# A transformer layer's feed-forward in seven products for each 2x2 grid of blocks, with activations spilled to DRAM

## The chip, the core and the metric

The kernel runs on one core of one Trainium2 chip. TensorE (PE) multiplies and writes PSUM, VectorE (DVE) and ScalarE (ACT) work elementwise, GpSimd (POOL) and SyncE (SP) mainly issue DMAs. The metric is device time in microseconds (us) of one execution. Lower is better.

## The reference

One layer of a diffusion backbone over 512 latent tokens and 256 context tokens of width 2048, all in float32. Cut to what matters:

```python
x = x + gt_m * (concatenate([hg_lat, at_lat], -1) @ w_out)       # mixers, output projection
h = modulate(rms_norm(x, norm_ffn_g), sh_f, sc_f)                # (512, 2048)
gate, up = split(h @ w_gate_up, 2, axis=-1)                      # w_gate_up (2048, 2 * 5632)
x = x + gt_f * ((silu(gate) * up) @ w_down)                      # w_down (5632, 2048)
```

Ahead of these lines stand the modulation (six rows of 2048 from silu(c) @ w_mod), a first norm, one input projection, a gated recurrence over eight heads and a windowed attention over eight heads. The change touches little of that.

## The kernel before

Every large product is made of three passes over fp32r operands. An operand a is split into a high part (rounded by ScalarE, function `split`) and a low part (a minus the high part, VectorE), and `mm3` adds high x high, high x low and low x high in one PSUM bank. PSUM has eight banks of 512 columns, four under the name mm and four under aux.

`Weights` loads weights in tiles of 512 KB on SP's DMA queue (tile wr), splits them in parts of 512 columns (wh, wl) and keeps a few parts ahead. `proj_a` multiplies activations (stationary) with weights (moving), a bank for each tile of 128 tokens; `proj_b` multiplies weights (stationary) with activations (moving, 512 tokens), a bank for each block of 128 columns. All products of the large projections are 512 columns wide, but for those of the context (256 tokens) and of the first gate of the feed-forward, which is made in two halves of 256 tokens.

Order of the stages: modulation and norm; context states of the recurrence; attention; recurrence of four pairs of heads; output projection in two halves of eight K chunks each, `add_gated` multiplying each bank by the gate (tile tm) and adding it to x1, which stays in SBUF (512 x 2048); the second norm `h2_half` for two tiles of tokens at a time (squares on ScalarE, a reciprocal root `rsqrt` of fourteen small VectorE steps, transposes on TensorE, modulation on ScalarE, split on VectorE); the feed-forward.

The feed-forward runs over blocks of two groups of 512 columns: gate (silu on ScalarE into sg), up (times sg, split into sa2), then down for all 2048 output columns in four parts of 512, each added to x1 with its gate. In the last block each finished tile of x1 is sent to the output. The four gate rows for it (tile gt_row) are made by `mod_row` in `mod_lane` during the first block: each is 16 VectorE operations on tiles m_w that SP loads, summed over partitions by one product.

Small work is woven into the products by `Lane`, which asks an estimate of the engines' clocks whether a next step may be issued. The framework that places instructions on the engines' queues may move an instruction ahead of others that it doesn't depend on; the trace shows the order that came out.

Of the kernel before, what the change touches and what calls it, by code (L numbers as in the profile page):

```python
# [9 lines left out]
F32 = mybir.dt.float32  # L10
# [8 lines left out]
P = 128  # L19
D = 2048  # L20
# [90 lines left out]
class Timed:  # L111
    """An engine whose calls are estimated."""
# [50 lines left out]
def tile_block(ctx: ExitStack, tc: tile.TileContext, x, c, ctx_in, c_ctx, w_mod, b_mod, norm_mix_g,  # L163
# [28 lines left out]
    gtm_d = dram.tile([1, D], F32, name="gtm_d")  # L192

    # ---------------------------------------------------------------- constants
# [12 lines left out]
    def rsqrt(tmp, v, shape, tag, eng=None, bufs=2):  # L207
        """1 / sqrt(v) by Newton's iteration from the usual bit-level seed."""
# [12 lines left out]
    # columns of small vectors: cols[d, j] = v[j * 128 + d]  # L221
# [40 lines left out]
    def lower_bounds(lt):  # L262
        """first row of a softmax over the layers; lbc[:, dir * 8 + head]"""
# [16 lines left out]
    # ---------------------------------------------------------------- products in three single passes  # L280
# [10 lines left out]
    class Weights:  # L291
        """Weight tiles [128, G, N] in the order of their use: loads and splits run ahead of the products."""
# [7 lines left out]
        def add(self, w, rows, c0, N, G):  # L300
            """G chunks of rows in a load, 512 columns in all in a split"""
# [14 lines left out]
        def ahead(self, upto):  # L316
            """splits issued for parts below upto, loads for as many more as there are buffers"""
# [54 lines left out]
    def proj_a(ws, rows, hT, toks, N, evac, before=None):  # L372
        """[tok, cols]: one bank for each tile of 128 tokens; rows: K chunks in order"""
# [15 lines left out]
    def proj_b(ws, hT, n_tok, N, evac, t0=0):  # L389
        """[cols, tok]: blocks of 128 columns, 512 / n_tok of them in a bank"""  # L390
# [22 lines left out]
    # ---------------------------------------------------------------- first part: modulation, h, keys and values  # L413
# [51 lines left out]
        # silu(c), silu(c_ctx)  # L465
# [144 lines left out]
    for grp in ff_blocks:  # L610
        for fg in grp:
            for c0 in (0, 0, D_FF) if fg == 0 else (0, D_FF):
                ws.add(w_gate_up, all_k, c0 + 512 * fg, 512, 2)
# [893 lines left out]
```

## Time and profile before

| | |
|---|---|
| time, median of 3 runs | 2664.23 us (2660.33 to 2671.72) |
| span of the profiled execution | 2664.4 us |
| TensorE busy | 2610.7 us, 98% |
| VectorE busy | 1494.4 us, 56% |
| ScalarE busy | 912.5 us, 34% |
| GpSimd busy | 89.1 us, 3% |
| read from and written to HBM | 368.5 MB and 14.7 MB |

The page gives the span alone for the profiled execution; it lies within 0.2 us of the median. A busy TensorE means that some product was in flight, not that products followed each other as fast as they can, so it is read together with the number of products in a stretch. Records of one product overlap with those of the next, so the price of a product is the distance between starts, not the mean length of a record.

### The profile page before, as it was taken

What the parts mean: (1) busy time and instruction counts of PE and PEld (TensorE: products, weight loads), DVE (VectorE), ACT (ScalarE), POOL (GpSimd) and SP (SyncE); (2) the same over time, 40 slices, a digit from 0 to 9 for tenths busy, and PEclk for the clock granted to TensorE, in tenths of its full rate; (3) what the DMA queues carried; (4) which work ended last, traced back from release to release, by engine and by line L of the source; (5) the groups of instructions that cost most, each with busy time, mean ns of one, the idle gap of its engine ahead of it and who ended that gap; (6) DMA issues with size and microseconds to landing.
All of it is one profiled execution on the core that took longest, in us unless ns stands there. A gap on an engine that the chain in (4) does not pass through costs nothing.

```text
span 2664.4 us, 33786 instructions
## 1 busy us (share of the span) xinstructions
PE 2610.7 (98%) x12495; PEld 2137.4 (80%) x12495; DVE 1494.4 (56%) x3085; ACT 912.5 (34%) x1781; POOL 89.1 (3%) x245
## 2 busy tenths in 40 slices
PE   7999999999999999999999999999999999999999
PEld 4579887878888878788788888888888888888887
DVE  4468967787888886567744333433353334233425
ACT  4245444447433343335222222222322222222222
POOL 0000010000011021000000000000000000000000
PEclk9999999999999999999999999999999999999999
DMA  9978677761323335546742332333223322332233
GB/s 345 319 258 268 217 234 223 231 193 59 113 81 102 98 119 190 165 139 202 243 139 96 95 95 95 99 99 95 95 95 96 97 98 97 95 95 95 96 103 111
DMA packets 230199, 385.36 MB, mean 145 GB/s; under 512 B 13201, under 2 KB 78898, under 8 KB 229266
## 3 DMA queue, kind: packets, MB, share of 16 engines
q1 hardware_dynamic: 210336, 354.48, 41.2%
q10 hardware_dynamic: 15682, 16.85, 1.9%
q0 software_dynamic: 4016, 11.88, 1.5%
q8 instruction: 98, 1.61, 0.2%
q14 instruction: 67, 0.55, 0.1%
HBM read 368.46 MB, written 14.69 MB: 144 GB/s over the span
## 4 chain that ended last, share of the span: by engine, by line
PE 84%; DVE 6%; DMA 4%; issue 3%; ACT 2%; POOL 1%; SPq 0%; ACTq 0%; DVEq 0%; POOLq 0%
PE mm L127 77%; PE aux L127 7%; DMA m_w<-in_w_mod_dram 2%; DVE wl L127 1%; DVE m_acc L127 1%; ACT hT L127 1%; DVE h L127 1%; DMA wr<-in_w_in_dram 0%; DMA mraw<-mix_d 0%; ACT wh L127 0%; DVE ce L127 0%; DMA ring<-in_ctx_dram 0%; POOL rs_t L127 0%; DVE tm L127 0%; DVE x L127 0%
## 5 line engine op out<-in xcount | busy, mean ns | idle before, releaser
L127 DVE TENSOR_TENSOR wl<-wr,wh 128x512 fp32r<-128x512 f32 x920 | 623.2, 688 | 904.7 <-PE mm L127 469.6
L127 ACT ACTIVATE wh<-wr 128x512 fp32r<-128x512 f32 x920 | 569.7, 630 | 1289.2 <-PE mm L127 1155.0
L127 PE MATMUL mm<-h,wh 128*128 128x512 f32 (+1 forms) x2944 | 880.6, 382 | 0.7 <-ACT wh L127 0.6
L127 PEld LDWEIGHTS mm<-h,wh 128*128 128x128 f32 x2944 | 544.0, 188 | 110.1 <-issue 1.7
L127 PE MATMUL mm<-h,wl 128*128 128x512 f32 (+1 forms) x1472 | 563.2, 383 | 1.8 <-DVE wl L127 1.8
L127 PE MATMUL mm<-wh,sa 128*128 128x512 f32 x1408 | 434.4, 389 | 0.0
L127 PEld LDWEIGHTS mm<-h,wl 128*128 128x128 f32 x1472 | 276.1, 188 | 61.0 <-DVE wl L127 2.5
L127 PEld LDWEIGHTS mm<-wh,sa 128*128 128x128 f32 x1408 | 264.3, 188 | 55.0
L127 PE MATMUL mm<-wh,hT 128*128 128x512 f32 x896 | 297.0, 402 | 3.0 <-ACT hT L127 3.0
L127 PE MATMUL mm<-wl,sa 128*128 128x512 f32 x704 | 273.9, 389 | 0.0
L127 PE MATMUL mm<-hT,wh 128*128 128x512 f32 x768 | 246.6, 397 | 0.0
L127 DVE SCALAR_TENSOR_TENSOR m_acc<-m_w,c_col,m_acc 128x512 f32<-128x512 f32 x240 | 179.6, 748 | 60.8 <-DMA m_w<-in_w_mod_dram 58.6
L127 PEld LDWEIGHTS mm<-wh,hT 128*128 128x128 f32 x896 | 169.2, 189 | 54.7 <-issue 8.6
L127 PE MATMUL mm<-wl,hT 128*128 128x512 f32 x448 | 178.4, 398 | 0.0
L127 PE MATMUL mm<-wh,mT 128*128 128x512 f32 x512 | 165.4, 398 | 4.2 <-DVE gsig L127 2.3
L127 PEld LDWEIGHTS mm<-hT,wh 128*128 128x128 f32 x768 | 142.2, 188 | 28.3
L127 PEld LDWEIGHTS mm<-wl,sa 128*128 128x128 f32 x704 | 132.2, 188 | 27.5
L127 PE MATMUL mm<-hT,wl 128*128 128x512 f32 x384 | 151.9, 396 | 0.0
L127 PEld LDWEIGHTS mm<-wh,mT 128*128 128x128 f32 x512 | 96.9, 189 | 28.5 <-DVE tm L127 4.1
L127 PEld LDWEIGHTS mm<-wl,hT 128*128 128x128 f32 x448 | 84.7, 189 | 24.0 <-issue 6.1
L127 PE MATMUL mm<-wl,mT 128*128 128x512 f32 x256 | 101.0, 394 | 0.0
L127 PE MATMUL mm<-cT,wh 128*128 128x256 f32 x512 | 93.5, 284 | 0.5 <-ACT wh L127 0.5
(251 smaller groups left out, 2301.9 us busy)
## 6 DMA issues: line engine op xcount, KB each, us to landing
wr<-in_w_gate_up_dram SPq DMA_DIRECT2D x184, 512.0 KB, 3.5
wr<-in_w_in_dram SPq DMA_DIRECT2D x144, 512.0 KB, 4.4
m_w<-in_w_mod_dram SPq DMA_DIRECT2D x128, 512.0 KB, 4.6
wr<-in_w_down_dram SPq DMA_DIRECT2D x88, 512.0 KB, 3.6
ring<-in_w_mod_dram SPq DMA_DIRECT2D x64, 512.0 KB, 8.8
wr<-in_w_out_dram SPq DMA_DIRECT2D x36, 512.0 KB, 4.2
wr<-in_w_in_dram ACTq DMA_DIRECT2D x16, 256.0 KB, 6.0
ring<-in_x_dram SPq DMA_DIRECT2D x4, 1024.0 KB, 8.8
```

Of the source, the lines that this page charges most:

```text
L127: return f(*a, **k)
```

## The change

The feed-forward is written anew by the Winograd form of Strassen's scheme. The grid for gate and up: tokens in two halves of 256, K in two halves of 1024, columns in gate and up (the two halves of w_gate_up). A group is 256 columns of both, there are 22; it takes eight steps (K chunk s of the first half with chunk s + 8 of the second), and each step makes seven products of blocks, `PRODUCTS`, each as 2 x 3 passes of 256 columns, into seven PSUM banks. For that VectorE makes four sums of the four weight blocks in three operations (`st_sums`), ScalarE the high parts of seven blocks (`st_high`, 1792 elements a partition), VectorE the low parts (`st_low`). The raw weights have three buffers (tag fx, shared with the raw activations xa), high and low parts three each. The activations are turned by f32 products with a diagonal of the norm (`turn`), summed and split (`form`) beside the first group. `evac_up` combines the seven banks, takes the silu, multiplies, makes sums and parts of the result for down and writes them to DRAM (sf_d, on POOL's queue).

Down does the same over 22 K chunk pairs, in four spans of 6, 6, 5 and 5 steps, for four column parts each; the sets come back from sf_d into eight buffers as these become free. `evac_down` combines seven banks and writes the part into y_d in DRAM: the first span writes, the second and third add by DMA, the last one adds in SBUF what `prepare_down` made of y_d, x1 and the gate, and sends the result out.

Ahead of it: x1 is also written to DRAM (x1_d), the squares of the second norm are taken in `add_gated` on ScalarE, the norm waits for all four tiles of tokens, and the four gate rows of the feed-forward join the earlier `mod_tasks` (buffer m_r single, in its own pool) and are stored in gtf_d. `h2_half`, the feed-forward's `Weights` and its lane work are gone.

```diff
+SC = 256
+N_UP = D_FF // SC
+SPANS = (6, 6, 5, 5)
+    def mod_gate(j, c0, dst):
+        t = est.tile(mp, [P, 512], F32, "m_r", "m_r", 1)
+        yield from mod_row(mp, c0 + 512 * j, t)
+        pool.dma_start(dst[0:1, 512 * j:512 * j + 512], t[0:1, :])
+        yield
+    mod_tasks += [mod_gate(j, 5 * D, gtf_d) for j in range(4)]
...
             dve.tensor_tensor(tm, bank, gate, op=ALU.mult)
+            dve.tensor_tensor(x1[j][:, t, :], x1[j][:, t, :], tm, op=ALU.add)
+            if squares:
+                act.activation(tm, x1[j][:, t, :], AF.Square, accum_out=ssj[:, t, j:j + 1])
+                if t == NT - 1:
+                    pool.dma_start(x1_d[:, 512 * j:512 * j + 512].rearrange("(t p) d -> p t d", p=P), x1[j])
...
+    PRODUCTS = ((0, 0), (2, 2), (5, 5), (3, 4), (1, 6), (4, 3), (6, 1))
+    def st_load(i):
+            u.x = est.tile(fx, [P, 8, SC], F32, "fx", "fx", 3)
+            for h in range(2):
+                sp_q.dma_start(u.x[:, 2 * h:2 * h + 2, :], u.src[h])
+    def st_sums(i):
+            dve.tensor_tensor(xx[:, 4:6, :], xx[:, 0:1, :].to_broadcast([P, 2, SC]), xx[:, 1:3, :], op=ALU.add)
+            dve.tensor_tensor(xx[:, 6, :], xx[:, 4, :], xx[:, 2, :], op=ALU.add)
+            dve.tensor_tensor(xx[:, 7, :], xx[:, 6, :], xx[:, 3, :], op=ALU.add)
+    def st_high(i):
+            u.hi = est.tile(fx, [P, 7, SC], F32R, "fh", "fh", 3)
+            act.activation(u.hi, u.x[:, 1:8, :], AF.Copy)
+    def st_low(i):
+            u.lo = est.tile(fx, [P, 7, SC], F32R, "fl", "fl", 3)
+            dve.tensor_tensor(u.lo, u.x[:, 1:8, :], u.hi.bitcast(F32), op=ALU.subtract)
...
+    def turn(s, h):
+        if h == 0:
+            xa[s] = est.tile(fx, [P, 8, SC], F32, "fx", "fx", 3)
+        kc = s + 8 * h
+        pt = aux_bank()
+        for n, t in enumerate((2, 3, 0, 1)):
+            pe.matmul(pt[:, n * P:(n + 1) * P], x1[kc // 4][:, t, (kc % 4) * P:(kc % 4 + 1) * P], diag[:, t, :],
+                      start=True, stop=True, skip_group_check=True)
+        act.activation(xa[s][:, 2 * h:2 * h + 2, :], pt.rearrange("p (h t) -> p h t", h=2), AF.Identity,
+                       bias=ab2[:, 1, kc:kc + 1], scale=ab2[:, 0, kc:kc + 1])
+    def form(s):
+        new_set(s)
+        a_sums(xa[s])
+        act.activation(sets[s][0], xa[s][:, 1:8, :], AF.Copy)
+        dve.tensor_tensor(sets[s][1], xa[s][:, 1:8, :], sets[s][0].bitcast(F32), op=ALU.subtract)
+    def evac_up(g, banks):
+        p1, p2, p6, p7, q4, q5, p3 = banks
+        e = est.tile(xg, [P, 4, 512], F32, "big", "big", 4)
+        r, u0, t, u1 = (e[:, k, :] for k in range(4))
+        act.activation(r, p1, AF.Copy)
+        dve.tensor_tensor(u0, p2, r, op=ALU.add)
+        dve.tensor_tensor(r, p6, r, op=ALU.add)
+        dve.tensor_tensor(t, r, p7, op=ALU.subtract)
+        dve.tensor_tensor(u1, t, q4, op=ALU.add)
+        dve.tensor_tensor(r, q5, r, op=ALU.subtract)
+        dve.tensor_tensor(t, q5, t, op=ALU.subtract)
+        dve.tensor_tensor(r, p3, r, op=ALU.add)
+        act.activation(t, t, AF.Silu)
+        act.activation(r, r, AF.Silu)
+        yield
+        dve.tensor_tensor(xx[:, 0:4:2, :], hf(t), hf(u1), op=ALU.mult)
+        dve.tensor_tensor(xx[:, 1:4:2, :], hf(r), hf(u0), op=ALU.mult)
+        yield
+        a_sums(xx)
+        act.activation(hl[0], xx[:, 1:8, :], AF.Copy)
+        yield
+        dve.tensor_tensor(hl[1], xx[:, 1:8, :], hl[0].bitcast(F32), op=ALU.subtract)
+        for i in range(2):
+            pool.dma_start(sf_d[2 * g + i].bitcast(F32), hl[i].bitcast(F32).rearrange("p f n -> p (f n)"))
+        yield
...
+    def evac_down(j, b, banks):
+        def done(k):
+            if fin:
+                dve.tensor_tensor(ck, ck, gt[:, n:n + 1, :].to_broadcast([P, 2, SC]), op=ALU.mult)
+                dve.tensor_tensor(c[:, k, :], c[:, k, :], z[:, k, :], op=ALU.add)
+                sp_q.dma_start(rows_of(out, h, n, j), ck)
+            elif b == 0:
+                pool.dma_start(rows_of(y_d, h, n, j), ck)
+            else:
+                pool.dma_start(rows_of(y_d, h, n, j), ck, accum_op=ALU.add)
...
+    for i, u in enumerate(steps):
+        st_load(i + 3)
+        st_sums(i + 2)
+        st_high(i + 2)
+        if i < 8:
+            hooks = {0: lambda: turn(i + 1, 0), 3: lambda: turn(i + 1, 1)}
+        run_step(i, hooks)
+        form(i + 1)
+        st_low(i + 2)
+        if not u.up and u.b == len(SPANS) - 1 and u.first:
+            tail.append(prepare_down(u.g))
+        for g in list(tail):
+            if next(g, tail) is tail:
+                tail.remove(g)
+        if u.last:
+            g = evac_up(u.g, u.banks) if u.up else evac_down(u.g, u.b, u.banks)
+            next(g)
+            tail.append(g)
+        if last_use[u.a] == i and pending:
+            n = pending.pop(0)
+            new_set(n)
+            for k in range(2):
+                pool.dma_start(sets[n][k].bitcast(F32).rearrange("p f n -> p (f n)"), sf_d[2 * (n - 8) + k].bitcast(F32))
```

## Rows read from the trace of the kernel before

**Rows 1.** The page's first lines, with busy time, share and instructions.

```profile
span 2664.4 us, 33786 instructions
PE 2610.7 (98%) x12495; PEld 2137.4 (80%) x12495; DVE 1494.4 (56%) x3085; ACT 912.5 (34%) x1781; POOL 89.1 (3%) x245
```

**Rows 2.** Windows: us, busy (count) of each engine, PEclk, DMA share, GB/s.

```profile
0.00:100.00 100.00, 83.12 (x471) 48.99 (x471) 47.85 (x125) 38.64 (x61) 1.16 (x7) 0.97 1.03 345
700.00:800.00 100.00, 97.95 (x475) 82.69 (x474) 90.46 (x256) 36.18 (x77) 12.09 (x34) 0.98 0.29 90
900.00:1000.00 100.00, 96.08 (x468) 79.79 (x468) 85.66 (x217) 39.35 (x90) 14.92 (x42) 0.98 0.35 109
1600.00:2000.00 400.00, 400.00 (x1756) 329.45 (x1755) 153.50 (x229) 105.78 (x170) 0.00 (x0) 1.00 0.30 97
1194.00:2660.00 1466.00, 1460.07 (x6594) 1206.77 (x6592) 618.69 (x980) 407.61 (x667) 0.00 (x0) 1.00 0.34 111
```

**Rows 3.** Timeline of TensorE between output projection and feed-forward.

```profile
1190.82 0.39 PE L127 MATMUL mm<-wh,mT 128*128 128x512 f32 x1
1192.95 2.23 PE L127 MATMUL aux<-ident,xn 128*128 128x128 f32 x16 [1.74 <-issue]
1194.98 1.01 PE L127 MATMUL mm<-h,wh 128*128 128x256 f32 x3
```

**Rows 4.** Timeline of TensorE, the context's projections: start, us, work merged.

```profile
224.74 0.40 PE L127 MATMUL mm<-cT,wh 128*128 128x256 f32 x2
228.63 0.40 PE L127 MATMUL mm<-cT,wh 128*128 128x256 f32 x2
235.13 1.02 PE L127 MATMUL aux<-m_acc,ones 128*128 128x512 f32 x2
236.22 0.28 PE L127 MATMUL mm<-cT,wl 128*128 128x256 f32 x1
```

**Rows 5.** Groups with shapes apart: busy us, mean ns, idle before, releaser.

```profile
L127 DVE TENSOR_TENSOR wl<-wr,wh 128x512 fp32r<-128x512 f32 x920 | 623.2, 688 | 904.7 <-PE mm L127 469.6 <-ACT wh L127 434.1
L127 DVE TENSOR_TENSOR h<-h,h 128x256 fp32r<-128x256 f32 x32 | 12.4, 416 | 0.1
L127 ACT ACTIVATE wh<-wr 128x512 fp32r<-128x512 f32 x920 | 569.7, 630 | 1289.2 <-PE mm L127 1155.0 <-DMA wr<-in_w_in_dram 37.8 <-PE aux L127 35.9
L127 ACT ACTIVATE xn<-x 128x2048 f32<-128x2048 f32 x4 | 7.6, 1911 | 0.0
L127 DVE SCALAR_TENSOR_TENSOR m_acc<-m_w,c_col,m_acc 128x512 f32<-128x512 f32 x240 | 179.6, 748 | 60.8 <-DMA m_w<-in_w_mod_dram 58.6
```

**Rows 6.** Timeline of VectorE: independent and dependent operations in sequence.

```profile
774.98 0.41 DVE L127 TENSOR_TENSOR ky<-hf,ky 128x256 f32<-128x256 f32 x1
775.32 0.41 DVE L127 TENSOR_TENSOR ky<-kx,hP 128x256 f32<-128x256 f32 x1
...
1179.00 0.69 DVE L127 TENSOR_TENSOR tm<-mm,gt_c 128x512 f32<-128x512 f32 x1
1179.73 0.69 DVE L127 TENSOR_TENSOR x<-x,tm 128x512 f32<-128x512 f32 x1
1180.35 0.69 DVE L127 TENSOR_TENSOR wl<-wr,wh 128x512 fp32r<-128x512 f32 x1
```

**Rows 7.** Timeline of VectorE inside the reciprocal root of the second norm.

```profile
1186.03 0.16 DVE L127 TENSOR_TENSOR rs_t<-rs_y 128x2 f32<-128x2 f32 x1
1186.11 0.68 DVE L127 TENSOR_TENSOR wl<-wr,wh 128x512 fp32r<-128x512 f32 x1
1186.71 0.15 DVE L127 TENSOR_TENSOR rs_t<-rs_t,ss 128x2 f32<-128x2 f32 x1
```

**Rows 8.** Window of TensorE: us, busy (count), PEclk, DMA share, GB/s.

```profile
420.00:440.00 20.00, 16.58 (x71) 0.88 0.68 216
```

**Rows 9.** DMA issues: out, in, engine, count, KB each, median us to landing.

```profile
wr<-in_w_gate_up_dram SPq DMA_DIRECT2D x184, 512.0 KB, 3.5
```

**Rows 10.** Timeline of VectorE, the last operation.

```profile
2660.53 0.69 DVE L127 TENSOR_TENSOR x<-x,tm 128x512 f32<-128x512 f32 x1
```

More of the change, by code (lines that the diff above doesn't have):

```diff
@@ L609, in tile_block @@
             ws.add(w_out, mix_order[8 * half:8 * half + 8], 512 * j, 512, 2)
[L610 to L613, printed above, removed]
-        for j in range(4):
-            ws.add(w_down, [4 * grp[0] + k for k in range(4 * len(grp))], 512 * j, 512, 2)
     ws.ahead(1)
@@ L1328, in tile_block @@
     m_st = ExitStack()
+    gp = m_st.enter_context(tc.tile_pool(name="gp", bufs=1))
     mT = mix_pools(m_st, 0)
@@ new lines, in tile_block @@
+    load_gate(gp, 0)
+    fx = ctx.enter_context(tc.tile_pool(name="fx", bufs=1))
+    ss2 = fx.tile([P, NT], F32, name="ss2")
+    diag = est.tile(fx, [P, NT, P], F32, "gtr", "diag", 1)
+    PRODUCTS = ((0, 0), (2, 2), (5, 5), (3, 4), (1, 6), (4, 3), (6, 1))
+    class Step:
+        pass
+    steps = []
+    for g in range(N_UP):
+        for s in range(8):
+            u = Step()
+            u.up, u.g, u.a, u.first, u.last = True, g, s, s == 0, s == 7
+            u.src = [w_gate_up[(s + 8 * h) * P:(s + 8 * h + 1) * P, :].rearrange("p (u n) -> p u n", u=2)
+                     [:, :, SC * g:SC * g + SC] for h in range(2)]
+            steps.append(u)
@@ L1394, in before @@
             if s == 4:
-                load_gate(j + 1)
-        proj_a(ws, list(range(8)), mT, NT, 512, add_gated(j, gts[j]), before)
-    last = add_gated(3, gts[3])
+                load_gate(gp, j + 1)
+        proj_a(ws, list(range(8)), mT, NT, 512, add_gated(gp, j, True), before)
+    mod_lane.drain()
+    for i in range(3):
+        st_load(i)
+    last = add_gated(gp, 3, True)
     proj_a(ws, list(range(8)), mT, (0, 1), 512, last)
-    lane.add(h2_half(0))
+    for i in range(2):
+        st_sums(i)
+        st_high(i)
+        st_low(i)
@@ new lines, in run_step @@
+    def run_step(i, hooks):
+        u = steps[i]
+        ah, al = sets[u.a]
+        if u.first:
+            n = sum(v.last for v in steps[:i])
+            u.banks = [(mm_bank if (n + k) % 2 == 0 else aux_bank)() for k in range(7)]
+        else:
+            u.banks = steps[i - 1].banks
+        for k, (fa, fb) in enumerate(PRODUCTS):
+            if k in hooks:
+                hooks[k]()
+            for b in range(2):
+                w = [v[:, fb, b * P:(b + 1) * P] if u.up else v[:, fb, :] for v in (u.hi, u.lo)]
+                a = [v[:, fa, :] if u.up else v[:, fa, b * P:(b + 1) * P] for v in (ah, al)]
+                mm3(u.banks[k][:, b * SC:(b + 1) * SC], *((w, a) if u.up else (a, w)), start=u.first, stop=u.last,
+                    first=u.first and b == 0)
@@ new lines, in tile_block @@
+    turn(0, 0)
+    turn(0, 1)
+    form(0)
+    pending = list(range(8, 8 + sum(SPANS)))
+    last_use = {u.a: i for i, u in enumerate(steps)}
+    tail = []
+    for i, u in enumerate(steps):
+        st_load(i + 3)
+        st_sums(i + 2)
+        st_high(i + 2)
+        hooks = {}
+        if i < 8:
[17 more added lines that the diff above has]
+                pool.dma_start(sets[n][k].bitcast(F32).rearrange("p f n -> p (f n)"), sf_d[2 * (n - 8) + k].bitcast(F32))
```

202 lines of the change are left out of this document (101 added, 101 removed).

## The prediction

> **What bounds the kernel now.** I read the busy time per engine first: TensorE is busy for 98% of a span of 2664.4 us [rows 1]. A busy TensorE only shows that something is always in flight, so the table by stretches comes next. There the reader is to see TensorE's count against the time: from 1600 to 2000 us 1756 products pass in 400 us, VectorE busy 153.5 and ScalarE 105.8 of the 400 [rows 2]. So the feed-forward runs at 400/1756 = 0.2278 us for a product of 512 columns and waits for no one. By the code it issues 6144 of them (gate and up 4032, down 2112) and 384 of 256 columns (the first gate, in two halves); the stretch 1194 to 2660 counts 6594 with the transposes [rows 2]. 6144 x 0.2278 + 384 x 0.1179 = 1445 us. The last product of the output projection starts at 1190.8 [rows 3], so the feed-forward and its tail own 2664.4 - 1191 = 1473 us. Only fewer or cheaper products shorten this, and only while no other engine takes over.
>
> The span and the median of the runs (2664.23) are the same to 0.2 us; the sum below is made against the span and holds for the median.
>
> **The products.** Seven instead of eight for each 2x2 grid, all 256 columns wide: up 22 x 8 x 7 x 2 x 3 = 7392, down 88 x 7 x 2 x 3 = 3696, together 11088. Their price stands in the trace: from 224.74 to 228.63, where the context is projected with 256 columns, eleven triples take 3.89 us, 0.1179 us a product [rows 4]. 11088 x 0.1179 = 1307 us, 138 less than 1445. A product of 512 costs only 0.2278, so halving the width alone gives back 3.5% of the eighth.
>
> The Trainium skill, page "TensorE: Matmul & The Clock Gate", section "Back-to-back issue gap", gives N/2.4 + 2.5 ns, so 109.2 for 256 columns. By it the new products would take 1211 us, by the row 1307. It puts 512 columns at 215.8 ns, where this trace has 227.8; the trace decides.
>
> **VectorE per step of the new loop.** Rows give 416 ns for 256 elements a partition and 688 for 512 [rows 5], 1.06 ns an element. Followed start to start, 256 take 0.34 us, 512 take 0.62, and 0.73 if an operation needs the one just before it (the pair that begins at 1179.00) [rows 6]. The three sums of a step are 0.62 + 0.45 + 0.45 = 1.52 (the last two depend on the one before). The low part of 1792 elements is 0.688 + 1280 x 1.06 ns - 0.07 = 1.98. Together 3.50 us a step, against 42 x 0.1179 = 4.95 on TensorE. A group of the up part has 8 steps (28.0), seven combinations out of PSUM (7 x 0.62 + 3 x 0.11 = 4.67), two products (1.24), sums (1.52) and the low part (1.98): 37.4 of 39.6 us, 94%. Before, VectorE was busy for 38% of such a stretch. ScalarE goes from 630 ns for 512 to 1911 for 2048 [rows 5], so 1.70 for 1792, some 17 us a group, and has room.
>
> What is late next? PSUM: seven of eight banks hold a group, so product k+1 of the next group's first step needs the bank of the former product k. Each product takes 0.71 us, VectorE frees a bank per 0.62 to 0.73, and the combinations begin while the last step still runs; the banks come in time unless VectorE is over 3 us late. Weights in parts are held for three steps, so VectorE may be late by about one step.
>
> No row shows this loop. The nearest are the recurrence's stretches: VectorE busy 90.5 and 85.7 of 100 us, TensorE 98.0 and 96.1 [rows 2]. So 2 to 4% of TensorE's time is lost at such a load. I take 3% of the up part (25 us) and 1.5% of the first three spans of down (5): 30. Ends: 10 and 75 (6% everywhere).
>
> **The beginning.** After the last product of the output projection the chain is serial, since the norm now needs all four token tiles: tm 0.73, x1 0.69, square and its accumulator 0.82, reduction 0.2, fifteen small steps at 0.2 (0.16 and a hand-over [rows 7]), diag 0.7, four f32 products of 128 columns, two activations of 0.7 (0.63 in [rows 5], and two operands), sums 1.5, high 1.7, low 2.05. An f32 product of 512 columns begins at 235.13, and the third of the next triple at 236.22 [rows 4]; less two spacings that is 0.85, so 0.21 for 128 and 0.85 for four. Sum 13.7, with some ten hand-overs of 0.1 us, 15. Before, four microseconds lay between those two stages, with sixteen transposes in them [rows 3]. The granted clock was 0.88 in a stretch with TensorE busy 16.6 of 20 us [rows 8], so part of such a stretch ran at the lower of its two levels; after 15 idle us I add 3.
>
> In the first eight steps the activations of step i+1 are turned, summed and split too: 0.7 + 0.85 + 0.7 + 1.52 + 1.70 + 2.05 and six hand-overs, 8.1 us, and the next round waits for its end because the three raw buffers are shared with the weights and leave one. VectorE has 7.0 us of work in it, so the chain decides: 7 x 8.1 + 4.95 = 62 instead of 39.6: +22 (15 to 35).
>
> **Moved work.** Four gates of the feed-forward go from 1200-1350 to before it. Each is 16 operations of 748 ns [rows 5], 48 us on VectorE in all, and 32 weight loads on SP ahead of the projection's own, with four broadcasts on POOL whose single buffer makes POOL wait with the recurrence's loads behind it. The lane issues them only where VectorE is not ahead of its budget, and from 1000 on it has room; the squares go to ScalarE. Cover gone, part of the 48 would show: 0 to 20, I take 5.
>
> **DRAM traffic.** A step loads 512 KB of weights, a group writes 1.8 MB: 152 GB/s, against 345 where the DMA engines were full [rows 2]. A load lands after 3.5 us [rows 9] and has two steps for it. At the end of up and in three stretches of down, 22 sets of 1.8 MB are read back, one a step: 2.36 MB at 345 GB/s is 6.8 us against 4.95. If nothing buffers that, 22 x 1.9 = 42 us; two steps of weights are held, so most of each stretch's 11 to 15 us is covered: 12 (0 to 42). The adds into DRAM stand off every chain until the last span, where the sum is read back.
>
> **The end.** In the last span VectorE has per block 5 x 3.5 + 4.67 + 8 x 0.62 + (4 x 0.62 + 2.25) = 31.9 against 24.8 on TensorE: it becomes the bound. 4 x 31.9 less 7 us of work done ahead is 121 against 99, and that holds most of the tail; with the last output 24. Before, the last operation began at 2660.53 [rows 10], some 5 us from the last product to the end.
>
> **Sum.** 1307 + 15 + 3 + 22 + 30 + 5 + 12 + 24 = 1418 instead of 1473: 1191 + 1418 = 2609, forecast 2610, 2% faster.
>
> **Rivals.** (a) VectorE becomes the bound and it is slower. In the code each step's low part stands behind its own sums on VectorE, and between them ScalarE's high part takes 1.7 us and two hand-overs, 1.9. If VectorE sits that out, a group takes 37.4 + 8 x 1.9 = 52.6 us, the whole some 2985. VectorE has only (39.6 - 37.4)/8 = 0.27 us a step to spare, so from 0.7 us of waiting a step the old time is reached; at 1.2 it is 2780. Against it: the queue isn't the code's order. The code writes the steps of the reciprocal root in one run, yet the trace has a weight split at 1186.11 between two of them [rows 7], so free work is drawn into such waits, and the next step's sums are free. For it: that order is fixed beforehand, and a load that lands late then holds all that stands behind it.
> (b) The read-back costs its full 42 us: 2640. For it, rows of weights are 1 KB and those of the sets 7 KB, with both kinds queued at once.
> The Trainium skill, page "DMA: Bandwidth & Descriptors", section "Queues, rings and completion order", says that a DMA engine changes between queues at whole packets; that would give the larger rows more than their turn. No run here shows it.
> (c) Almost no loss, every bound at its lower end: 1307 + 15 + 15 + 10 + 12 = 1359, so 2550.
> (d) The narrow products cost more in this mix than in the context's stretch: 11 us a nanosecond, and 5 ns undo it, 2665. Against it, eleven triples in a row keep that pace [rows 4].
>
> **How the numbers follow.** Forecast 0.50, (a) 0.23, (b) 0.11, (c) 0.12, (d) 0.04. Half a per cent, 13 us, is about what a measurement of this kernel can tell from no change. Faster: all of (c), nearly all of the forecast and of (b), 0.69; same 0.08; slower, most of (a) and half of (d), 0.23. The range reaches from the lower end (c), 2545, into (a) up to 2720, where the wait is 0.9 us a step.
>
> **What would show it.** TensorE's triples of 256 columns at 0.354 us; a group of the up part in 40 to 41 us with VectorE busy near 37; the first group some 62; 15 to 18 us without a product before it; in the last span VectorE without gaps. A wait of the low part for the high part, repeated in every step and over 0.7 us, would prove (a); waits for the weight loads only where sets are read back, (b).

## The result, and the profile after

The changed kernel takes 2723.69 us (2719.01 to 2729.11), the kernel before beside it on the same chip 2662.28: 1.0228 times as long, with a 95% interval of 1.0205 to 1.0252. It is slower by 2.3% where 2% faster was forecast, and lies just above the range's upper end of 2720. The profiled execution has a span of 2719.6 us.

The page's first lines answer to [rows 1]: TensorE is busy for 53 us less than before, in a span that is 55 us longer.

```profile
span 2719.6 us, 44137 instructions
PE 2557.2 (94%) x17119; PEld 2317.3 (85%) x17119; DVE 2119.3 (78%) x3706; ACT 1060.6 (39%) x1529; POOL 219.9 (8%) x429
```

The windows of the changed kernel, with the columns of [rows 2] (us, busy and count of PE, PEld, DVE, ACT and, where it is there, POOL; granted clock, DMA share, GB/s):

```profile
600.00:1000.00 400.00, 382.08 (x1868) 313.95 (x1867) 349.84 (x969) 170.36 (x399) 52.41 (x141) 0.98 0.41 126
1600.00:2000.00 400.00, 400.00 (x3336) 400.00 (x3335) 353.25 (x447) 168.00 (x120) 10.69 (x20) 1.00 0.47 152
2100.00:2130.00 30.00, 30.00 (x252) 30.00 (x251) 25.70 (x34) 13.58 (x10) 0.41 (x1) 1.00 0.43 137
2130.00:2145.00 15.00, 13.74 (x115) 13.54 (x113) 6.23 (x11) 3.35 (x3) 2.24 (x5) 1.00 0.94 350
2145.00:2155.00 10.00, 1.69 (x8) 1.69 (x9) 5.66 (x6) 1.25 (x1) 2.65 (x5) 0.68 0.34 132
2155.00:2190.00 35.00, 25.61 (x172) 24.99 (x171) 13.56 (x16) 7.61 (x6) 4.21 (x8) 0.80 0.90 339
2581.00:2710.00 129.00, 111.57 (x843) 108.28 (x842) 113.75 (x151) 33.11 (x24) 28.18 (x38) 0.91 0.55 166
```

The second line is the new loop as it should be: TensorE without a gap, 3336 products in 400 us, VectorE busy 88%. The three lines from 2130 are the place where sets are first read back: the DMA engines are at 0.90 to 0.94, 339 to 350 GB/s, and between two such stretches TensorE works 1.7 of 10 us while the DMA engines are at 0.34. The last line is down's last span: VectorE is busy for 113.8 of 129 us, and 843 products take 111.6 us of TensorE, 0.132 each, at a granted clock of 0.91.

TensorE's timeline between the output projection and the feed-forward answers to [rows 3]: the last product of the one starts at 1223.01 (1190.82 before), the first of the other at 1238.99.

```profile
1223.01 0.39 PE L130 MATMUL mm<-wh,mT 128*128 128x512 f32 x1
1230.71 4.40 PE L130 MATMUL aux<-diag,x 128*128 128x128 f32 x24 [7.31 <-issue]
1238.99 0.58 PE L130 MATMUL mm<-a,fh 128*128 128x256 f32 x1 [3.88 <-ACT a L130]
```

The DMA issues of the page (out, in, queue, count, KB each, median us to landing), to be read against [rows 9]; over the whole kernel weight loads, now of 256 KB, land after 3.3 and 3.7 us (3.5 for the 512 KB before), and the read-back `a<-sf_d` takes 9.8 us:

```profile
fx<-in_w_gate_up_dram SPq DMA_DIRECT2D x352, 256.0 KB, 3.3
fx<-in_w_down_dram SPq DMA_DIRECT2D x176, 256.0 KB, 3.7
sf_d<-big POOLq DMA_DIRECT2D x44, 896.0 KB, 4.1
a<-sf_d POOLq DMA_DIRECT2D x44, 896.0 KB, 9.8
```

The same list for 2130 to 2190 alone shows what a median hides: there weight loads of 256 KB land after 6.0 and 13.0 us in the median.

```profile
a<-sf_d POOLq DMA_DIRECT2D x16, 896.0 KB, 8.9
fx<-in_w_down_dram SPq DMA_DIRECT2D x8, 256.0 KB, 6.0
fx<-in_w_gate_up_dram SPq DMA_DIRECT2D x5, 256.0 KB, 13.0
```

Of the waits from 1190 us on (engine, what it waited for: us in total, times, longest), the two longest of VectorE, both for weight loads, and the longest of TensorE:

```profile
DVE fx L130 <- DMA fx<-in_w_down_dram: 105.9, 32, 11.2
DVE fx L130 <- DMA fx<-in_w_gate_up_dram: 77.0, 67, 12.8
PE aux L130 <- DVE fl L130: 42.1, 10, 9.6
```

Not all of VectorE's waiting is loss: from 1600 to 2000 it waits 18.4 us for loads, and TensorE for nothing. TensorE itself never waits for a set that is read back; from 2123 to 2581 its waits all end on VectorE. The longest, 9.6 us up to 2153.3, shows how a late load reaches it. VectorE's timeline (start, length, operation, idle before and releaser):

```profile
2148.70 0.69 DVE L130 TENSOR_TENSOR fx<-fx 128x512 f32<-128x512 f32 x1 [7.78 <-DMA fx<-in_w_gate_up_dram]
2149.30 2.02 DVE L130 TENSOR_TENSOR big<-big 128x1792 fp32r<-128x1792 f32 x1
2151.24 2.02 DVE L130 TENSOR_TENSOR fl<-fx,fh 128x1792 fp32r<-128x1792 f32 x1
```

The load ends the wait at 2148.7, a low part of the activations (`big`) goes first, and only behind it comes the low part of the weights that TensorE needs. The products that follow start 0.21 us apart until 2158.6, against 0.12 before the stop.

The prediction's sum, set against the start of each group's and span's first product in TensorE's timeline (us):

| stretch | predicted | measured | difference |
|---|---|---|---|
| up to the last product of the output projection | 1191 + 5 | 1223.0 | +27 |
| from there to the first product of up | 15 + 3 | 16.0 | -2 |
| first up group | 62 | 77.0 | +15 |
| the next 20 up groups | 792 + 24 of loss | 807.1 (40.3 each) | -9 |
| last up group, down, tail | 41 + 436 + 5 + 12 + 24 | 65.1 + 521.8 + 9.5 | +78 |
| all | 2610 | 2719.5 | +109 |

Down's four spans of 6, 6, 5 and 5 steps took 136.3, 136.6, 120.1 and 128.8 us, where the products alone need 121, 121, 101 and 101 at 0.12 us. In several runs with unaltered code ahead of the feed-forward, the output projection ended between 1214.6 and 1226.7; differences of 12 us there aren't an edit's. The first up group, with unaltered code, took 72.2 to 80.0 us, by and large the longer the lower its granted clock was (0.93 to 0.81).

### The profile page after: what moved, and what is told of

Read it like the earlier page. It is cut to its first block, busy times and chain, and to the rows that moved or that the text cites. A ratio compares the mean times of both kernels' runs of the same rounds, so it can differ in the third digit from the quotient of the medians.

```text
span 2719.6 us, 44137 instructions
## 1 busy us (share of the span) xinstructions
PE 2557.2 (94%) x17119; PEld 2317.3 (85%) x17119; DVE 2119.3 (78%) x3706; ACT 1060.6 (39%) x1529; POOL 219.9 (8%) x429
## 4 chain that ended last, share of the span: by engine, by line
PE 32%; DMA 9%; DVE 8%; issue 2%; SPq 1%; ACT 0%; DVEq 0%; ACTq 0%
PE mm L130 16%; PE aux L130 16%; DMA fx<-in_w_down_dram 7%; DVE fl L130 4%; DVE big L130 3%; DVE fx L130 2%; DMA fx<-in_w_gate_up_dram 1%; SPq L130 1%; DMA gtr<-gtf_d 0%; ACT fh L130 0%; DVEq L130 0%; ACTq L130 0%
## 5 line engine op out<-in xcount | busy, mean ns | idle before, releaser
L130 ACT ACTIVATE fh<-fx 128x1792 fp32r<-128x1792 f32 x264 | 448.0, 1701 | 739.4 <-DVE fx L130 291.5
L130 DVE TENSOR_TENSOR fl<-fx,fh 128x1792 fp32r<-128x1792 f32 x264 | 532.6, 2019 | 60.6 <-ACT fh L130 58.9
L130 DVE TENSOR_TENSOR fx<-fx 128x256 f32<-128x256 f32 (+1 forms) x816 | 409.5, 510 | 213.3 <-DMA fx<-in_w_down_dram 105.9
L130 PE MATMUL mm<-a,fh 128*128 128x256 f32 x2464 | 478.6, 285 | 13.5 <-ACT a L130 12.1
L130 PE MATMUL aux<-a,fh 128*128 128x256 f32 x2464 | 475.4, 284 | 1.0 <-ACT fh L130 1.0
L130 PEld LDWEIGHTS mm<-a,fh 128*128 128x128 f32 x2464 | 388.9, 192 | 15.2 <-ACT a L130 13.0
L130 PEld LDWEIGHTS aux<-a,fh 128*128 128x128 f32 x2464 | 387.8, 191 | 1.3 <-ACT fh L130 1.2
L130 PE MATMUL aux<-a,fl 128*128 128x256 f32 x1232 | 351.6, 285 | 18.8 <-DVE fl L130 18.8
L130 PE MATMUL mm<-a,fl 128*128 128x256 f32 x1232 | 351.1, 285 | 0.0
L130 DVE TENSOR_TENSOR wl<-wr,wh 128x512 fp32r<-128x512 f32 x376 | 251.1, 685 | 89.0 <-ACT wh L130 88.3
L130 PEld LDWEIGHTS mm<-fh,a 128*128 128x128 f32 x1232 | 218.3, 198 | 19.5 <-DVE big L130 14.9
```

The source lines that it names most:

```text
L130: return f(*a, **k)
```

## The experiments

"Under the changed kernel" compares medians. The kernel before, run beside each set of experiments, had medians from 2659.3 to 2663.2, so differences of 4 us between medians of different sets say nothing; there the ratios decide.

**No read-back.** Down takes the sets that up left in the buffers; its input is therefore wrong, and the 39 MB are written but not read.

```diff
-            new_set(n)
-            for k in range(2):
-                pool.dma_start(sets[n][k]..., sf_d[2 * (n - 8) + k]...)
+            sets[n] = sets[u.a]
```

> Leaves out the read-back: down multiplies the activations that up left in the eight buffers, nothing is read from sf_d; it is still written. Theory R (the 22 sets read back hold up the weight loads): last group of up back from 65 to 40-42 us, down from 522 to 450-465, whole 2640 to 2660. Rival D (VectorE and the adds into DRAM hold down up): the blocks of down keep their times, whole above 2705.

2638.30 us, ratio 0.9922 [0.9896, 0.9948], 85 us under the changed kernel. The last up group is 40.3, the spans 121.8, 119.6, 102.6 and 127.0: all but the last are the products' own time. Last group, down and tail are 520.8 in place of 596.4, so 76 us are the read-back's; the rest of the 85 lies ahead, where the profiled runs differ anyway. Of some 74 us in the last group and the first three spans, 50 are time in which TensorE stood still, and 23 are slower products (405.5 us for 3193 at a granted clock of 0.94, against 382.1 for 3195 at 1.00). Theory R held, but down took 471.0, over its 450 to 465: the last span stays, so something else holds it. Its window:

```profile
2500.00:2622.00 122.00, 106.81 (x799) 103.15 (x798) 109.55 (x143) 31.93 (x21) 28.23 (x38) 0.90 0.58 175
```

VectorE is busy for 90% of it, which points at VectorE without proving it.

**No gates.** The four gate rows of the feed-forward are the bias alone; their 64 operations and 32 weight loads are gone, the output is scaled wrongly.

```diff
-    mod_tasks += [mod_gate(j, 5 * D, gtf_d) for j in range(4)]
+    pool.dma_start(gtf_d[0:1, :], b_mod[5 * D:6 * D][None, :])
```

> Leaves out the products behind the four gate rows of the feed-forward (the bias alone is stored). Theory M (the moved gates cost the recurrence what TensorE lost ahead of the feed-forward): the output projection ends at 1191 to 1196 instead of 1223, whole 2692 to 2700. Rival P (the squares and the copy of x1 at the output projection cost it): no change, 2715 to 2728.

2698.44 us, ratio 1.0136 [1.0112, 1.0161], 25 us under the changed kernel; the output projection ends at 1198.9, 24 us sooner and 3 us past theory M's range. So the moved tasks account for some 24 of the 32 us by which it ended later than in the kernel before; the other 8 no run takes apart. Where they run is seen in windows that count only the operations on the accumulator m_acc (us; busy and count of PE, PEld, DVE); first the kernel before, then the changed one:

```profile
1250.00:1400.00 150.00, 4.18 (x8) 1.43 (x8) 42.70 (x58) 1.00 0.61 200
```

```profile
600.00:800.00 200.00, 4.06 (x12) 1.85 (x12) 34.48 (x48) 0.98 0.45 139
800.00:1000.00 200.00, 2.05 (x4) 0.68 (x4) 11.64 (x16) 0.97 0.37 114
```

Before, they lay in the feed-forward, where VectorE had 62% to spare [rows 2]; now they lie in the recurrence, whose window from 600 to 1000 us passes 1868 products instead of the 1947 of the kernel before.

**Gates later.** The same tasks from the output projection's second column step on.

```diff
-    for g in mod_tasks:
+    for g in mod_tasks[:12]:
...
+        if j == 1:
+            for g in mod_tasks[12:]:
+                mod_lane.add(g)
```

> The tasks of the MLP gate's columns (with their 256 KB weight loads and their m_acc operations) are no longer queued beside the recurrence but from the second column step of the output projection on, where the kernel before had them; everything else is the changed kernel. Theory M (the 32 us by which the output projection ends later, 1223.0 against 1190.8, are the price of where these tasks run, not of the tasks): it ends at 1192 to 1205 and the whole takes 2692 to 2706. Rival T (the tasks cost that anywhere, since VectorE must do them): it ends at 1215 or later and the whole is 2715 to 2724, as without the edit.

2719.87 us, ratio 1.0215 [1.0192, 1.0239]; the output projection ends at 1228.2. T held, and M fell: beside the output projection they cost what they cost beside the recurrence. In the trace 16 of the 64 operations still lie at 688 to 705 us; 48 moved. (The expectation has one error: the kernel before ran them a little further on, in the first part of the feed-forward.)

**Order of issue.** The reads of a set are popped at every second step.

```diff
-        if last_use[u.a] == i and pending:
+        if last_use[u.a] == i:
+            free += 1
+        if free and pending and i % 2 == 1:
+            free -= 1
```

> The same sets are read back, one every second step instead of one a step. Theory R1 (the trouble is the burst, 2.36 MB a step): 1.44 MB a step is 286 GB/s, so most of the loss goes, whole 2665 to 2690. Rival R2 (any read-back starves the weight loads for as long as it lasts, however far apart): the loss is only spread, 2710 to 2728.

2717.52 us, ratio 1.0205 [1.0184, 1.0225], last up group 65.2. The run doesn't tell the theories apart: GpSimd issued the reads in the same rhythm as before (from 2126.5, 2130.7 and 2149.4 us on, against 2129.6, 2133.7 and 2152.4), so nothing was paced.

**Rows of 1 KB.** The spilled sets lie in DRAM so that a read has rows of 1 KB, like the weights, in place of 7 KB.

```diff
-    sf_d = dram.tile([2 * N_UP, P, 7 * SC], F32R, name="sf_d")
+    sf_d = dram.tile([2 * N_UP, 7, P, SC], F32R, name="sf_d")
...
```

> sf_d is laid out so that each row that is written or read back is 1 KB, as the weights' rows are, instead of 7 KB. Theory S (shares go by packets, so 7 KB rows take most of the engines): weight loads beside a read-back land in 7 to 9 us instead of 13.5, whole 2680 to 2705. Rival B (only the sum of bytes counts): within 8 us of 2724, or slower by less efficient rows.

2727.23 us, ratio 1.0248 [1.0219, 1.0278]. The last up group fell to 57.2, but the first block of each of the first three spans took 46.2, 45.5 and 40.3 us; between 2130 and 2190 weight loads land after 11.7 to 12.5 us. The size of the rows only moved the loss.
The Trainium skill's "DMA: Bandwidth & Descriptors", section "Queues, rings and completion order", on which rival (b) leaned (an engine changes queues at whole packets), is neither refuted nor needed by this: with equal rows the weights waited as long.

**Paced reads.** GpSimd copies one column of a weight part that is made two steps ahead into the set's buffer before it reads, half a set a step; so the read really waits.

```diff
+        if freed and i + 2 < len(steps):
+            n, k = freed.pop(0)
+            if k == 0:
+                new_set(n)
+            pool.tensor_copy(sets[n][k][:, 0, 0:1], steps[i + 2].lo[:, 0, 0:1])
+            pool.dma_start(sets[n][k]..., sf_d[2 * (n - 8) + k]...)
...
```

> The read-back of the spilled activations is paced: GpSimd waits for a weight set that is prepared two steps ahead before it issues the next half set (896 KB), so the reads are spread over the last up group and all of down's first spans instead of coming in one burst. Bytes are the same 39 MB. Theory R1 (the burst is what costs: weight loads queue behind it): last up group 40 to 45, the first two span sums 122 to 126, third 103 to 110, the whole 2640 to 2665. Rival R2 (the bytes cost, wherever they are read): the loss of about 85 us is spread out and the whole stays at 2700 to 2730. One of between, 2670 to 2700, if the adding of a wait for the sets hurts the start of down, where up's buffers come free late.

2704.21 us, ratio 1.0145 [1.0108, 1.0182]. The last up group is 43.6 as R1 said, but the first block of down takes 54.2 us, and the spans 147.3, 129.1, 118.0 and 135.8. Of the 56 us that last group and first two spans had over the run without reads (338.0 against 281.7), 18 came back. From 2130 to 2190 the reads of this run land sooner, the weights hardly (2155 to 2225 shows VectorE waiting 19.6 us for them, and TensorE 7.3 for a set):

```profile
a<-sf_d POOLq DMA_DIRECT2D x9, 896.0 KB, 6.6
fx<-in_w_down_dram SPq DMA_DIRECT2D x14, 256.0 KB, 5.7
fx<-in_w_gate_up_dram SPq DMA_DIRECT2D x4, 256.0 KB, 9.7
```

Moving the bytes in time helps little; R2 is nearer.

**Half the bytes.** The seven combinations are spilled once, unsplit, and split behind the read.

```diff
+        pool.dma_start(sf_d[g], xx[:, 1:8, :].rearrange("p f n -> p (f n)"))
...
+            hi, lo = sets[v.a]
+            act.activation(hi, lo.bitcast(F32), AF.Copy)
+            dve.tensor_tensor(lo, lo.bitcast(F32), hi.bitcast(F32), op=ALU.subtract)
```

> The seven combinations of an activation block are spilled once, as f32, and not as a high and a low part: 19.7 MB are written and read back in place of 39.5 MB. They land in the buffer of the low part; ScalarE and VectorE split them there two steps ahead of their first use (22 times 1.7 us and 2.0 us, which evac_up loses). Theory B (the bytes of the read-back are what down loses, in the way of its weight loads): of the 85 us that the run without the read-back gave, half or more comes back: last up group 40 to 50, span sums 122 to 130, 120 to 130, 103 to 112, 125 to 131, the whole 2645 to 2685, so one to three hundredths of the time under the changed kernel. Rival V (VectorE's 2.0 us a block in down cost as much as the bytes give): 2700 or more. Under pure proportion to the bytes: 2677 to 2685.

2672.68 us, ratio 1.0040 [1.0025, 1.0054], 51 us under the changed kernel. Last up group 42.7, spans 125.2, 131.2, 110.4 and 133.2: 22 us gone in the last group and 22 in down, 44 of the read-back's 76 with half the bytes. Theory B held, though the second and the last span lie 1 to 2 us over its ranges; rival V did not show. The edit also takes the split out of up's last steps and puts it into down, so it isn't a test of the bytes alone.

```profile
fx<-in_w_down_dram SPq DMA_DIRECT2D x176, 256.0 KB, 3.6
a<-sf_d POOLq DMA_DIRECT2D x22, 896.0 KB, 6.9
```

**Plain writes.** Down's parts are written to y_d without adding; the sum is incomplete.

```diff
-                pool.dma_start(rows_of(y_d, h, n, j), ck, accum_op=ALU.add)
+                pool.dma_start(rows_of(y_d, h, n, j), ck)
```

> Down's parts of the spans behind the first are written plainly to y_d instead of being added there, so y_d holds only the last part and the second half of the output is not the full sum. All bytes, sizes and issues stay but the read that an adding transfer makes at its target. Theory A (the adds, which land after 5.6 to 8 us where plain writes take 3.6, delay the sum buffers and through them TensorE): the four spans of down fall by 10 us or more in all, the whole to 2700 to 2713. Rival N (the adds are hidden, as the prediction had them): 2716 to 2727, with span sums within 3 us of 136, 137, 120 and 129.

2713.81 us, ratio 1.0196 [1.0174, 1.0217]; the spans are 137.7, 134.5, 120.3 and 123.1. In the three spans that write or add nothing changed by more than 2 us; the 6 us of the last, which reads y_d back, is all there is. The adds are hidden in those three, as N says. The whole lies between the two ranges, and the intervals of this run and of the changed kernel overlap.

**GpSimd prepares the last span.** The four multiplications and the addition of `prepare_down` move from VectorE (the expectation counts two).

```diff
-            dve.tensor_tensor(hf(z[:, k, :]), hf(z[:, k, :]), gt..., op=ALU.mult)
+            pool.tensor_tensor(hf(z[:, k, :]), hf(z[:, k, :]), gt..., op=ALU.mult)
...
-        dve.tensor_tensor(z, z, x1t, op=ALU.add)
+        pool.tensor_tensor(z, z, x1t, op=ALU.add)
```

> The three operations that prepare the second half of the output (gate times part, twice, and the addition of the residual), which ran on VectorE in down's last span, run on GpSimd. Theory V (the last span's 128 us against 101 us of products is VectorE's work, as predicted at 31.9 us a block): the last span falls to 105 to 118, the whole to 2706 to 2716. Rival G (the last span waits for transfers, of y_d's parts or of weights): it stays at 125 to 130 and the whole at 2716 to 2727, or is longer, where GpSimd is slower in the same place.

2727.96 us, ratio 1.0250 [1.0223, 1.0277]; the last span took 136.1. That is rival G's number, but not its reason. The groups with shapes apart (engine, operation, out, in, shapes, count, busy us, mean ns, idle before) in the last span, first of the changed kernel:

```profile
L130 DVE TENSOR_TENSOR fl<-fx,fh 128x1792 fp32r<-128x1792 f32 x20 | 39.8, 2017 | 0.0
L130 DVE TENSOR_TENSOR fx<-fx 128x256 f32<-128x256 f32 x36 | 14.4, 417 | 0.1
L130 DVE TENSOR_TENSOR big<-mm,big 128x512 f32<-128x512 f32 x11 | 7.4, 684 | 5.7 <-PE mm L130 5.7
```

and with GpSimd at work:

```profile
L130 DVE TENSOR_TENSOR fl<-fx,fh 128x1792 fp32r<-128x1792 f32 x19 | 44.3, 2354 | 1.8 <-ACT fh L130 1.7
L130 POOL TENSOR_TENSOR big<-big,gtr 128x512 f32<-128x512 f32 x16 | 34.9, 2589 | 7.0 <-DMA gtr<-gtf_d 7.0
L130 DVE TENSOR_TENSOR fx<-fx 128x256 f32<-128x256 f32 x34 | 29.9, 893 | 0.6
L130 DVE TENSOR_TENSOR big<-mm,big 128x512 f32<-128x512 f32 x11 | 7.4, 685 | 3.6 <-PE mm L130 3.6
```

VectorE's own sums of 256 elements went from 417 to 893 ns. What was taken off it came back as longer operations, so the run decides nothing on V. The waits of the changed kernel's last span say more: TensorE stood still for 17 us there, every time for VectorE or for ScalarE's high parts, and VectorE waited 8 us for transfers (6.2 for weights, 2.0 for the gate's row).

**A fourth raw buffer**, on the kernel with half the bytes, for one high buffer less.

```diff
-            u.x = est.tile(fx, [P, 8, SC], F32, "fx", "fx", 3)
+            u.x = est.tile(fx, [P, 8, SC], F32, "fx", "fx", 4)
...
-            u.hi = est.tile(fx, [P, 7, SC], F32R, "fh", "fh", 3)
+            u.hi = est.tile(fx, [P, 7, SC], F32R, "fh", "fh", 2)
```

> As the kernel with the unsplit spill, with a fourth raw buffer (fx), paid for with one of the three high buffers. Theory C (the first up group takes 77 us against 40 because weights and turned activations share three raw buffers, so the turn of the next block waits for the low part of the one before): first group 50 to 64, everything behind it as without, the whole 13 to 27 us under the kernel with the unsplit spill. Rival H (the chain turn, ScalarE, sums, high, low of one block is itself longer than TensorE's 5 us): first group 72 or more. Two high buffers would show as up groups above 40.3. A fourth weight buffer could also bring some us in down's first spans, where weight loads land late.

2696.47 us, ratio 1.0120 [1.0103, 1.0137], 24 us over the kernel that it stands on. The first group took 80.1 against 75.2, so C's gain didn't come; that one high buffer fewer hid it isn't excluded. Some up groups grew to 41.7, the last one to 48.8, which the two high buffers may have cost; no run has them alone.

**Gates inside the up groups**, on the kernel with half the bytes: one m_acc operation a step, weights into a big tile, one product for the sum in every fourth group.

```diff
+        if k == 2:
+            gacc["w"] = est.tile(xg, [P, 4, 512], F32, "big", "big", 4)
+            pool.dma_start(gacc["w"], w_mod[512 * c4:512 * c4 + 512, c0:c0 + 512]...)
+        if k >= 4:
...
+                dve.scalar_tensor_tensor(gacc["a"], w, cc, gacc["a"], op0=ALU.mult, op1=ALU.add)
```

> As the kernel with the unsplit spill, and the MLP gate's four column groups are formed inside the up groups (1 MB weight loads into a big tile on GpSimd's queue, one m_acc operation a step in the second half of a group, their sum by one product every fourth group), where VectorE stood idle for 12 of 100 us. Theory S (64 operations of 0.75 us fit into that slack): output projection ends at 1196 to 1205, up groups 40.3 to 41.5 with 4 of 42 to 45, the whole 12 to 24 us under the kernel with the unsplit spill. Rival T (they cost the same 25 us here as beside the recurrence and beside the output projection): the whole within 5 us of it.

2660.63 us, ratio 0.9988 [0.9973, 1.0003], 12 us under the kernel with half the bytes. The output projection ends at 1194.3, and from the first product of up to the first of down 936.0 us pass in place of 924.3. Of these 11.7 us, 4.8 lie in the first group, which has none of the tasks; the twenty middle groups took 812.8 in place of 806.4. So theory S holds at its lower end: of the 20 us that the output projection gained, a third to a half shows again in up.

**All three together.**

> The three edits together: unsplit spill, fourth raw buffer, the MLP gate's columns inside the up groups. If they act at different places (theories B, C and S), their gains add: 2610 to 2650, under the kernel before. If two of them draw on the same slack of VectorE, the sum falls short by 10 us or more. If only the spill counts: 2645 to 2685.

2686.81 us, ratio 1.0092 [1.0056, 1.0128]: the edit that gained and the one that lost add up on the kernel with half the bytes (2672.68 - 12 + 24 = 2685). The 2610 to 2650 expected took the fourth buffer for a gain.

**The last span without its preparation**, on the kernel with half the bytes and the gates inside up: the residual stream is the output's first content, and each part is multiplied by the gate and added there by DMA.

```diff
-        dve.tensor_tensor(z, z, x1t, op=ALU.add)
...
-                dve.tensor_tensor(c[:, k, :], c[:, k, :], z[:, k, :], op=ALU.add)
-                sp_q.dma_start(rows_of(out, h, n, j), ck)
+            dve.tensor_tensor(ck, ck, prepared[0]..., op=ALU.mult)
+            pool.dma_start(rows_of(out, h, n, j), ck, accum_op=ALU.add)
```

> As the kernel with the unsplit spill and the gate's columns inside the up groups. The residual stream is written to the output in DRAM as its first content, every part of down is multiplied by the gate (2.7 us of VectorE a block) and added to the output by DMA, in all four spans: the reads, the multiplications and the additions that prepared the last span (7.7 us of VectorE a block there) are gone, and 2.7 us a block are new in the first three spans. Theory V (the last span is VectorE's): it falls from 131 to 105 to 115, the spans before change by -3 to +8 each, the whole to 2632 to 2655, under the kernel before. Rival G (the last span waits for transfers): it stays at 125 or more, or the adding transfers, which land later than plain writes, make it longer, and the whole is 2655 to 2680.

2657.77 us, ratio 0.9996 [0.9981, 1.0011]. The last span fell from 130.7 to 110.8, as V says. Its windows (columns as above), first of the kernel that this one stands on:

```profile
2519.00:2650.00 131.00, 112.53 (x839) 108.91 (x839) 114.40 (x153) 34.04 (x23) 29.28 (x39) 0.91 0.55 165
```

```profile
2533.00:2645.00 112.00, 104.14 (x840) 102.67 (x840) 94.89 (x124) 34.44 (x25) 25.74 (x25) 0.95 0.56 128
```

VectorE's work fell by 19.5 us and the span by 19.9, at the same DMA share. The reads of y_d and x1 went with it, so the run alone doesn't part V from G; the waits above do. The granted clock rose from 0.91 to 0.95. The whole gained nothing that can be told (0.9988 for that kernel, 0.9996 for this one) and misses V's range by 3 us: the first three spans grew from 126.3, 131.3 and 114.5 to 133.2, 133.8 and 123.1, where the multiplication (2.7 us a block) is new, and the tail from 9.5 to 12.3.

**The second turn earlier**, on that kernel.

```diff
-            hooks = {0: lambda: turn(i + 1, 0), 3: lambda: turn(i + 1, 1)}
+            hooks = {0: lambda: turn(i + 1, 0), 2: lambda: turn(i + 1, 1)}
```

> As the run before, and in the first up group the second turn of the next activation block is put behind the second of seven products instead of the third (0.7 us of TensorE earlier in a step). If the chain turn, ScalarE, sums, high, low begins at that place (theory H), each of seven steps is about 0.7 us shorter and the first group 3 to 6 us; if VectorE's order sets the steps, the first group stays within 1.5 us of the run before.

2654.91 us, ratio 0.9978 [0.9967, 0.9989]: 0.2% under the kernel before, the one kernel here that leaves out no work and whose interval lies below 1. The first group fell from 75.9 to 67.4. ScalarE's timeline shows the chain that H names, in the changed kernel and here (start, length, operation, idle before and releaser); `fx<-aux,ab` is the second half of a turn:

```profile
1254.32 0.78 ACT L130 ACTIVATE fx<-aux,ab 128x512 f32<-128x512 f32 x1 [2.24 <-PE aux L130]
1256.84 1.70 ACT L130 ACTIVATE a<-fx 128x1792 fp32r<-128x1792 f32 x1 [1.74 <-DVE fx L130]
```

```profile
1226.22 0.78 ACT L130 ACTIVATE fx<-aux,ab 128x512 f32<-128x512 f32 x1 [1.56 <-PE aux L130]
1228.74 1.70 ACT L130 ACTIVATE a<-fx 128x1792 fp32r<-128x1792 f32 x1 [1.74 <-DVE fx L130]
```

The wait for TensorE is 0.7 us shorter, the rest of the chain the same. From one second half to the next it is 9.0 us on average in place of 9.6 in the run before, over five rounds; that is 3 of the 8.5 us, as H says. The rest lies in the group's first and last steps, and its granted clock was 0.97 against 0.87, so how much of it is the edit's stays open.

## Why the prediction was wrong, by its own steps

**DRAM traffic: the term that failed most.** It had 12 us (0 to 42); the run without the read-back shows 76. Its place and its first link were right (a set a step is more than the DMA engines bring beside the weights, and the loss shows as waits for weight loads). But it priced only the bytes of the reads and let two steps of weights absorb most of that; 42 was its most, with nothing absorbed. It left out what follows a late load: VectorE has to catch up with the parts while TensorE stands still, and the products behind the stop run slower, 23 us of the loss. And the loss outlasts the reads: not only the blocks that read sets grew (the last ones of the first three spans 39.8, 40.8 and 31.4 us, without reads 29.9, 29.9 and 26.6), but also the blocks behind them (the first ones 34.7, 33.9 and 33.4, without reads 29.6, 29.9 and 24.9). With half the bytes 32 us of the 76 remained, and spreading them gave 18, so more than half goes with the bytes. Rival (b) had the right place, with 42 us as its most.

**Moved work: 32 where 5 stood (0 to 20), 24 of them the gates'.** "From 1000 on it has room" was the error: the lane put the tasks into the recurrence, where VectorE was already busy 86 to 91% [rows 2], and put beside the output projection instead (48 of 64 operations) they cost the same. The cover that had hidden them was the old feed-forward's idle VectorE, and the change itself removed it.

**The first group: 77 where 62 stood (15 to 35 us over 39.6; measured 37 over).** The chain was the right one, its start was not: the second half of a turn stands behind the third product block of seven, so 1.9 us of products (1260.65 to 1262.54 in TensorE's timeline) come first, where the working had 0.7 for the first half's activation. A round took 9.6 us where 8.1 stood, 11 of the 15 us over seven rounds; the first and the last step have the rest, in a group whose granted clock was 0.83; the working took its prices from rows at full clock. Putting the second half one block earlier shortened a round by 0.6. The shared raw buffers, which the prediction held to be the reason for the serial rounds, had no part in it, as far as the run with a fourth (and one high buffer fewer) shows.

**The products: 0.1179 was 0.1199** (400/3336), 22 us over 11088. This is rival (d) in small, 2 ns of its 5.
The Trainium skill's "TensorE: Matmul & The Clock Gate", section "Back-to-back issue gap", comes to 109.2 ns by its formula, which it gives for a single product apart from its figures for a sustained stream; this loop is still further from it than the context's stretch was.

**Loss by VectorE: 30 where nearly none came.** The 20 middle groups take 40.3 us, which is 336 products at that price; VectorE was busy 88% there, not 94%, and no product waited. Rival (a), the one that carried the slower side, didn't happen: low parts waited for high parts, but for 58.9 us over 264 steps, 0.22 a step, less than the 0.27 that VectorE had to spare. The group of the low parts in the whole kernel (busy us, mean ns, idle before):

```profile
L130 DVE TENSOR_TENSOR fl<-fx,fh 128x1792 fp32r<-128x1792 f32 x264 | 532.6, 2019 | 60.6 <-ACT fh L130 58.9 <-PE mm L130 1.1
```

The result came out slower for other reasons; that it lies on (a)'s side of the range is no support for (a).

**The gap and the end held.** 16.0 against 18 us; the last span 128.8 us against 4 x 31.9 = 127.6 without work done ahead. That VectorE sets it is shown by its waits and by the run that took 7.7 us a block off it and put 2.7 back. That the number fits so closely is in part luck: VectorE was busy for 113.8 us, not 127.6, and not without gaps, and 10 us of the span are products slowed by the clock. The 7 us of work done ahead didn't come, and the tail was 9.5.

So of the 109 us, 64 are the read-back, 27 the stretch up to the output projection (the gates' 24 and the 8 left open, less the 5 that stood), 15 the first group; the price of the products and the loss by VectorE nearly cancel. The range failed because the two terms with open covers, the read-back and the moved work, were both bounded as if only what is moved could show, and not what it holds up. The lower clock behind a stop was counted once, 3 us at the gap, and nowhere else.

## What to carry over

Fewer products are worth what is left after everything that the old, wider loop hid: list what ran in its idle engines and idle DMA time, and price each at its full cost in the new place. Data spilled to DRAM is best spilled before it is expanded: splitting behind the read took half the bytes and gave 51 us. A stop of TensorE is priced with the slower products behind it. A chain between engines is timed from the place in the instruction order where its first link is issued, not from its first operation's length.

## What the runs showed of the hardware

With GpSimd reading and writing SBUF, VectorE's operations with both operands in SBUF grew (417 to 893 ns for 256 elements, 2017 to 2354 for 1792). They grew only beside a GpSimd operation: ten sums of 256 that ran wholly beside one took 2.02 us on average, the 23 beside none 0.42; seven low parts 2.93, the eight beside none 2.02. Of 31 operations with one operand in PSUM only two ran beside one, and kept their 0.69 us.
The Trainium skill's "SBUF — State Buffer", section "SBUF: two separate sides", says of VectorE operations with two SBUF inputs that they and a GpSimd operation that reads SBUF exclude each other; the trace agrees, for the operand in PSUM on two operations.

In 10 us with TensorE busy for 1.7 us, and in the 35 us behind it, the granted clock was 0.68 and 0.80, part of the time at the lower of its two levels; the 172 products of the 35 us took 0.149 us each in place of 0.120. Each stall for weights so cost more than its own length.
